# Weight sums of the 7-product blocks formed on VectorE instead of by accumulating transfers, with later transposes and another order of steps

## The chip, the cores and the metric

The kernel runs on one core of one Trainium2 chip, as one launch. The metric is the device time of that launch in microseconds (us), here the median of three runs. All data are fp32. The products use the fp32r form, in which each operand is split into a high part and the rest, so that one product of two tiles is three matmuls.

## The reference

Two transformer-like blocks run one after the other on 256 tokens of width 1024. Cut to what matters here:

```python
x = x + 0.5 * swiglu(rms_norm(x, g), w_gate, w_up, w_down)     # four of these, FF = 2816
x = x + mixer_1(x)        # sparse attention and pooling
x = x + mixer_2(x)        # spatial gating and short convolution
# order: swiglu, mixer_1, swiglu | swiglu, mixer_2, swiglu, final norm

def swiglu(x, w_gate, w_up, w_down):
    return (jax.nn.silu(x @ w_gate) * (x @ w_up)) @ w_down
```

The change touches the four swiglu stages, called FFN 1 to 4 below, and the choice of PSUM bank for transposes in the two mixers.

## The kernel before, in words

**An FFN stage** (`ffn`, L318) has three parts. The gate and up products are made for eleven groups of 256 columns, in pairs: five groups of 512 columns (numbers 0 to 4) and one of 256 (number 5). The gated result is transposed into the tile `act`, and the down product (`down`, L368) reads `act`.

**Weights come in chunks** of 128 x 2048 (1 MB). `weights` (L62) loads one through SP's queue into one of two `raw` buffers. `parts` and `split` (L70, L76) make the high part on ScalarE (ACT, `whi`, L77) and the rest on VectorE (DVE, `wlo`, L78). There are three buffers of each, so the splitting runs at most three chunks ahead of the matmuls. `mm3` (L80 to L85) then runs three matmuls per pair of tiles, on L83, L84 and L85. L84 is the first that needs `wlo`, and L85 the first that needs the low part of the activations. A plain chunk is 24 matmuls of 512 columns.

**Plain groups** (`eight`, L344) take a chunk per step. Group 5 takes two chunks and groups 2 and 4 take four. After the last one, `silu` runs on ACT (`sg`, L330) and `gated` multiplies on DVE (`pr`, L338). Then `turned` (L204) transposes `pr` on TensorE (L210) and splits the result into `act` on ACT and DVE. `turned` is put off by `later(f, n)`: each step of the order ends with `flush`, which takes 2 off n after a plain step and 1 after a block step, and runs f where nothing is left.

**Blocks of seven products** (`seven`, L358, and `quad`, L154) do groups 1 and 3. They multiply a 2 x 2 arrangement of weight chunks w11, w12, w21, w22 with seven products instead of eight. A product is 12 matmuls of 512 columns, one product per step. The activation sums are made once per FFN (`combined`, L133, which uses two of the four `block` buffers for its own data and splits into `xc`). Four weight sums are needed:

- w12 + w22 and w11 + w12: made by accumulating transfers (L175). A second DMA from HBM is added to the chunk that is in SBUF already. These and the plain loads of `block` (L151) are issued by GpSimd's (POOL's) queue.
- then + w22 and + w21 onto the latter: made on DVE (L192, L195).

`block` has four buffers, so the second block's loads wait until the first block gives buffers back, and the third and fourth load of the first block wait for `combined`.

**The order of the steps** is written out by hand in `ORDER` (L36): `e` is group 5, `a` the block of group 1, `2` and `4` the groups 2 and 4, `b` the block of group 3, `d` the down product. In what follows a1 to a7 and b1 to b7 are the steps of the blocks. The queue of each engine follows this order on the whole, but not strictly: an instruction may stand ahead of one of an earlier step.

**The end of an FFN's gate part:** the last act chunk (group 3) becomes ready last, so the first half of `down` takes its chunks in the order 0, 1, 2, 4, 5, 3 (L374). Chunk 5 is half as long.

**In the mixers** (`mixer1` L442, `mixer2` L695) `ps` (L58) goes round all eight PSUM banks, while `turned` and the transposes in `add` (`pair`, L266) take one of the three banks tagged `tmp`.

Of the kernel before, what the change touches and what calls it, by code (L numbers as in the profile page):

```python
# [13 lines left out]
ALU = mybir.AluOpType  # L14
# [3 lines left out]
P = 128  # L18
T = 256
# [13 lines left out]
MASKED = -1.0e30  # L33
WARM = 14

ORDER = "eaeaa2a2aa2a244bb4bb4bdbdbdddddddddd"  # L36


class Block:
# [14 lines left out]

    def bank(self, tag, shape=(P, 512)):
        return self.psum.tile(list(shape), F32, tag=tag, name=tag, bufs={"acc": 5, "tmp": 3}[tag])

    def ps(self, shape=(P, 512)):  # L58
        self.banks += 1
        return self.bank("acc" if self.banks % 8 < 5 else "tmp", shape)  # L60
# [93 lines left out]
    def quad(self, pool, b, x, xc):  # L154


        nc, tt = self.nc, self.nc.vector.tensor_tensor
        of_x = lambda c, t: lambda k: self.both(x[:, 4 * c + k, :, t * P : t * P + P])
        of_xc = lambda i: lambda k: self.both(xc[:, 4 * i + k, :, :])

        def product(left, w):
            ps = self.bank("tmp")
            for k in range(4):
                c = slice(k * 512, k * 512 + 512)
                self.mm3(ps, left(k), (w[0][:, c], w[1][:, c]), k == 0, k == 3)
            return ps

        p = lambda tag: pool.tile([P, 512], F32, tag=tag, name=tag)

        def copy(ps, tag):  # L170
            y = p(tag)
            nc.scalar.activation(y, ps, AF.Copy)
            return y

        more = lambda w, src: nc.gpsimd.dma_start(w, src, accum_op=ALU.add)  # L175
        (b11, b12), (b21, b22) = b
        w11, w12, w22, w21 = self.block(b11), self.block(b12), self.block(b22), self.block(b21)
        more(w12, b22)
        y11 = copy(product(of_x(0, 0), self.parts(w11)), "p1")
        more(w11, b12)  # L180
        yield
        p7 = copy(product(of_xc(2), self.parts(w12)), "p7")
        yield
        y12 = copy(product(of_xc(3), self.parts(w22)), "p3")
        yield
        y21 = p("p2")
        tt(y21, product(of_x(1, 0), self.parts(w21)), y11, op=ALU.add)
        y11, v = y21, y11
        yield
        p5 = copy(product(of_xc(0), self.parts(w11)), "p5")  # L190
        yield
        tt(w11, w11, w22, op=ALU.add)  # L192
        tt(v, product(of_xc(1), self.parts(w11)), v, op=ALU.subtract)
        yield
        tt(w11, w11, w21, op=ALU.add)  # L195
        w = self.parts(w11)
        ps = product(of_x(1, 1), w)
        tt(p7, p7, v, op=ALU.add)
        tt(v, v, p5, op=ALU.add)
        tt(p5, p7, p5, op=ALU.add)  # L200
        tt(p7, ps, p7, op=ALU.subtract)
        return y11, p7, y12, v, p5

    def turned(self, dst, x, k):  # L204

        for t in range(2):
            n = x[t].shape[1] // P
            pt = self.bank("tmp", (P, 4, P))
            for i in range(n):
                self.nc.tensor.transpose(pt[:, i, :], x[t][:, i * P : i * P + P], self.ident)  # L210
            s = slice(t * P, t * P + P)
            self.split(dst[:, k : k + n, 0, s], dst[:, k : k + n, 1, s], pt[:, :n, :])
# [37 lines left out]
    def add(self, accs, f, scale, following, tiles=(0, 1)):  # L250

        nc = self.nc
        s = slice(f * 512, f * 512 + 512)
        for t in tiles:
            x = self.X[t][:, s]
            nc.vector.scalar_tensor_tensor(x, accs[t], scale, x, op0=ALU.mult, op1=ALU.add)
        if following is None:
            return
        for t in tiles:
            self.squares(t, f)  # L260
        if following == "final_norm_2":
            return
        if f == 0:
            self.hT = self.big.tile([P, KD, 2, T], F32R, tag="hT", name="hT")

        def pair(k):  # L266
            pt = self.bank("tmp", (P, 2, T))
            for i in range(2):
                for t in range(2):
                    nc.tensor.transpose(pt[:, i, t * P : t * P + P], self.X[t][:, (k + i) * P : (k + i) * P + P], self.ident)  # L270
            for i in range(2):
                self.feed(k + i, pt[:, i, :], following)

        for k in (4 * f, 4 * f + 2):
            self.later(lambda k=k: pair(k), 3)
# [42 lines left out]
    def ffn(self, n, following, first=False):  # L318
        nc, a = self.nc, self.a
        gu, d, d_end = a[f"gu{n}"], a[f"d{n}"], a[f"de{n}"]  # L320
        with self.stage(4), self.tc.tile_pool(name="act", bufs=1) as pool:
            act = pool.tile([P, KF, 2, T], F32R, tag="act", name="act")
# [11 lines left out]
            def gated(j, sgs, us):  # L334
                prs = []
                for t in range(2):
                    pr = self.work.tile([P, 512], F32, tag="pr", name="pr", bufs=4)[:, : us[t].shape[1]]
                    nc.vector.scalar_tensor_tensor(pr, us[t], r[:, t : t + 1], sgs[t], op0=ALU.mult, op1=ALU.mult)  # L338
                    prs.append(pr)
                self.later(lambda: self.turned(act, prs, 4 * j), 2)  # L340

            two = lambda: [self.bank("acc") for _ in range(2)]

            def eight(j):  # L344
                G = two()
                self.token_major(G, gu[2 * j], 512, 0)
                yield
                self.token_major(G, gu[2 * j], 512, 1)
                sgs = silu([x[:, :T] for x in G] if j == 5 else G)
                if j < 5:  # L350
                    yield
                    U = two()
                    self.token_major(U, gu[2 * j + 1], 512, 0)
                    yield
                    self.token_major(U, gu[2 * j + 1], 512, 1)
                gated(j, sgs, [x[:, T:] for x in G] if j == 5 else U)

            def seven(j):  # L358
                y11, y21, y12, x, y22 = yield from self.quad(pool, [[gu[2 * j + i, c] for i in range(2)] for c in range(2)], self.hT, xc)

                def rest():
                    tt = nc.vector.tensor_tensor
                    tt(y12, y12, x, op=ALU.add)
                    gated(j, silu([y11, y21]), [y12, y22])

                self.later(rest, 3)

            def down():  # L368
                for f in range(2):
                    accs = two()  # L370
                    w = lambda c: self.weights(d[f, c] if c < 5 else d_end[f])
                    rows = lambda c, w, last, **k: self.rows(accs, w, act, 4 * c, 4 if c < 5 else 2, last, **k)
                    split = f == 1 and following == "final_norm_2"
                    order = (0, 1, 2, 4, 5, 3) if f == 0 else range(4 if split else 6)  # L374
                    for c in order:
                        if f or c:
                            yield
                        rows(c, w(c), 15 if f == 0 else KF - 1)
                    if split:
                        ws = [w(4), w(5)]  # L380
                        for t in range(2):
                            for c in (4, 5):
                                rows(c, ws[c - 4], KF - 1, tiles=[t])
                            self.add(accs, f, 0.5, following, [t])
                    else:
                        self.add(accs, f, 0.5, following)
# [12 lines left out]
            if not first:  # L399
                self.token_major(U, gu[1], 512, 1)  # L400
            gated(0, silu(G), U)
            combined = self.combined(xc, self.hT)
            next(combined)

            steps = {"a": seven(1), "b": seven(3), "2": eight(2), "4": eight(4), "e": eight(5), "d": down()}
            for step in ORDER:
                next(steps[step], None)
# [34 lines left out]
    def mixer1(self, following):  # L442
# [225 lines left out]
        def out(t, O):  # L668
# [4 lines left out]
            self.split(mT[0][:, :, 0, s], mT[0][:, :, 1, s], pt)  # L673

        ET = turned(0)
        pls = means()
        O = attend(0, ET)
        pooled(pls)
        ET = turned(1)
        mT[0] = self.m1.tile([P, 4, 2, T], F32R, tag="L1", name="mT")  # L680
        project(1, 0)
# [281 lines left out]
```

## Time and profile before

| what | us |
|---|---|
| median of three runs | 1137.19 (1135.1 to 1139.62) |
| profiled execution, its own time | 1135.03 |
| its span, first to last instruction | 1133.3 |
| TensorE busy with matmuls | 1081.6 |
| VectorE busy | 758.3 |
| ScalarE busy | 576.0 |

The busy time of TensorE includes overlap of one matmul with the next, so the distance between the starts of two matmuls says more than the length of one. The mean granted clock of TensorE over the span was 0.983 of full speed.

The FFNs lie at about 0 to 200, 305 to 505, 505 to 700 and 930 to 1133 us. In each, the first steps of the order begin some 25 us in.

### The profile page before, as it was taken

The page shows a single profiled execution, that of the slowest core. Times are in us where ns is not written, and L with a number is a line of the kernel's source. Part 1 is how long each engine was busy: PE and PEld are TensorE (multiplying, and loading weights), DVE is VectorE, ACT ScalarE, POOL GpSimd, SP SyncE. Part 2 cuts the span into 40 slices and gives each one's busy share as a digit, 9 for nine tenths or more (in the row PEclk, how much of TensorE's full clock was granted, in tenths as well). Part 3 has the DMA queues.
Part 4 walks back from the last instruction along what each step waited for, and adds up shares of the span by engine and source line. Part 5 has one row for each costly group of instructions (what it writes and reads, how often), then busy time and mean ns, then how long its engine had stood idle before and what let it go on. Part 6 is the DMA issues. An engine that isn't in the chain of part 4 may idle for free.

```text
span 1133.3 us, 12907 instructions
## 1 busy us (share of the span) xinstructions
PE 1081.6 (95%) x5182; PEld 900.8 (79%) x5182; DVE 758.3 (67%) x780; ACT 576.0 (51%) x657; POOL 51.2 (5%) x85
## 2 busy tenths in 40 slices
PE   9898999899998899999889999999999999889996
PEld 7677888778887688888768878999888878767885
DVE  6685875597575769646776855687545557666953
ACT  7545543577454464544646454533444445546442
POOL 1100000120010000001000000000000001000000
PEclk9999999999998999999989999999999999999999
DMA  9956365633386743659574565454545438674362
GB/s 355 284 176 226 112 231 187 251 112 113 112 290 192 259 115 132 224 188 313 179 260 112 206 229 208 175 189 174 184 176 178 169 120 281 201 253 119 130 223 74
DMA packets 34956, 218.54 MB, mean 193 GB/s; under 512 B 4609, under 2 KB 5009, under 8 KB 10321
## 3 DMA queue, kind: packets, MB, share of 16 engines
q1 hardware_dynamic: 26784, 164.20, 39.8%
q0 software_dynamic: 7680, 52.98, 16.1%
q8 instruction: 40, 0.66, 0.2%
q10 hardware_dynamic: 432, 0.55, 0.1%
q14 instruction: 20, 0.16, 0.0%
HBM read 216.66 MB, written 1.05 MB: 192 GB/s over the span
## 4 chain that ended last, share of the span: by engine, by line
PE 70%; DVE 10%; DMA 10%; issue 5%; ACT 4%; POOL 0%; SPq 0%; POOLq 0%; ACTq 0%; DVEq 0%
PE acc L85 16%; PE acc L83 16%; PE acc L84 16%; PE tmp L83 6%; PE tmp L84 6%; PE tmp L85 6%; DVE wlo L78 6%; DMA block<-in_gu 5%; DMA raw<-in_gu 4%; ACT whi L77 3%; PE tmp L210 2%; PE acc L91 1%; DMA raw<-in_d 1%; DVE xc L78 1%; DVE block L192 1%
## 5 line engine op out<-in xcount | busy, mean ns | idle before, releaser
L78 DVE TENSOR_TENSOR wlo<-raw,whi 128x2048 fp32r<-128x2048 f32 (+1 forms) x127 | 282.2, 2222 | 175.4 <-ACT whi L77 175.4
L77 ACT ACTIVATE whi<-raw 128x2048 fp32r<-128x2048 f32 (+1 forms) x127 | 236.3, 1860 | 244.3 <-PE acc L85 106.8
L78 DVE TENSOR_TENSOR wlo<-block,whi 128x2048 fp32r<-128x2048 f32 (+2 forms) x99 | 198.5, 2013 | 100.4 <-ACT whi L77 100.3
L85 PE MATMUL acc<-whi,hT 128*128 128x512 f32 (+1 forms) x608 | 238.1, 392 | 3.2 <-DVE hT L223 3.2
L83 PE MATMUL acc<-whi,hT 128*128 128x512 f32 (+1 forms) x608 | 240.0, 396 | 0.5 <-ACT whi L77 0.4
L84 PE MATMUL acc<-wlo,hT 128*128 128x512 f32 (+1 forms) x608 | 238.4, 392 | 1.3 <-DVE wlo L78 1.3
L77 ACT ACTIVATE whi<-block 128x2048 fp32r<-128x2048 f32 (+2 forms) x99 | 166.7, 1691 | 107.5 <-PE acc L85 27.3
L84 PE MATMUL acc<-wlo,act 128*128 128x512 f32 x352 | 137.1, 389 | 0.6 <-DVE wlo L78 0.6
L83 PE MATMUL acc<-whi,act 128*128 128x512 f32 x352 | 137.6, 391 | 0.0
L85 PEld LDWEIGHTS acc<-whi,hT 128*128 128x128 f32 x608 | 115.8, 190 | 27.0 <-DVE hT L223 3.6
L85 PE MATMUL acc<-whi,act 128*128 128x512 f32 x352 | 136.9, 392 | 0.1
L84 PEld LDWEIGHTS acc<-wlo,hT 128*128 128x128 f32 x608 | 116.0, 191 | 24.6 <-DVE wlo L78 2.1
L83 PEld LDWEIGHTS acc<-whi,hT 128*128 128x128 f32 x608 | 116.2, 191 | 24.3 <-ACT hT L222 0.8
L85 PEld LDWEIGHTS acc<-whi,act 128*128 128x128 f32 x352 | 66.1, 188 | 15.2 <-DVE act L78 1.6
L84 PEld LDWEIGHTS acc<-wlo,act 128*128 128x128 f32 x352 | 66.1, 188 | 14.6 <-DVE wlo L78 1.0
L83 PEld LDWEIGHTS acc<-whi,act 128*128 128x128 f32 x352 | 66.1, 188 | 13.3
L83 PE MATMUL tmp<-whi,hT 128*128 128x512 f32 x144 | 57.2, 397 | 4.3 <-ACT whi L77 4.3
L84 PE MATMUL tmp<-wlo,hT 128*128 128x512 f32 x144 | 56.2, 390 | 0.0
L85 PE MATMUL tmp<-whi,hT 128*128 128x512 f32 x144 | 56.1, 390 | 0.0
L84 PE MATMUL tmp<-wlo,xc 128*128 128x512 f32 x128 | 52.7, 412 | 1.6 <-DVE wlo L78 1.6
L83 PE MATMUL tmp<-whi,xc 128*128 128x512 f32 x128 | 53.5, 418 | 0.0
L210 PE MATMUL tmp<-ident,pr 128*128 128x128 f32 x176 | 27.9, 296 | 26.6 <-DVE pr L338 26.6
(249 smaller groups left out, 1390.6 us busy)
## 6 DMA issues: line engine op xcount, KB each, us to landing
raw<-in_gu SPq DMA_DIRECT2D x52, 1024.0 KB, 4.9
block<-in_gu POOLq DMA_DIRECT2D x48, 1024.0 KB, 8.5
raw<-in_d SPq DMA_DIRECT2D x40, 1024.0 KB, 4.8
raw<-in_de SPq DMA_DIRECT2D x8, 512.0 KB, 3.5
block<-in_w_out SPq DMA_DIRECT2D x4, 1024.0 KB, 4.9
raw<-in_w_out SPq DMA_DIRECT2D x4, 1024.0 KB, 5.1
block<-in_w_cx SPq DMA_DIRECT2D x4, 1024.0 KB, 4.9
raw<-in_w_cx SPq DMA_DIRECT2D x4, 1024.0 KB, 5.0
```

Source lines behind the costliest of these rows:

```text
L77: self.nc.scalar.activation(hi, x, AF.Copy)
L78: self.nc.vector.tensor_tensor(lo, x, hi.bitcast(F32), op=ALU.subtract)
L83: mm(ps, lhsT=a[0], rhs=b[0], start=start, stop=False)
L84: mm(ps, lhsT=a[0], rhs=b[1], start=False, stop=False)
L85: mm(ps, lhsT=a[1], rhs=b[0], start=False, stop=stop)
L91: self.nc.tensor.matmul(ps, lhsT=a, rhs=b, start=start, stop=stop)
L192: tt(w11, w11, w22, op=ALU.add)
L210: self.nc.tensor.transpose(pt[:, i, :], x[t][:, i * P : i * P + P], self.ident)
```

## The change

The two accumulating transfers of each block are gone. The sums w11 + w12 and w12 + w22 are formed by two DVE instructions directly after the first product's split, and w12 is loaded first. The transposes of a gated result are put off by 4 instead of 2. The order of the steps runs both chunks of group 5 ahead of the first block's first product and spreads the blocks' steps otherwise. In the mixers, transposes take a bank from the round of eight.

```diff
-ORDER = "eaeaa2a2aa2a244bb4bb4bdbdbdddddddddd"
+ORDER = "eeaa2a2aa2a2a44bb4b4bbdbdbdddddddddd"
...
+    def side(self, shape):
+        return self.ps(shape) if self.spare else self.bank("tmp", shape)
...
-        more = lambda w, src: nc.gpsimd.dma_start(w, src, accum_op=ALU.add)
         (b11, b12), (b21, b22) = b
-        w11, w12, w22, w21 = self.block(b11), self.block(b12), self.block(b22), self.block(b21)
-        more(w12, b22)
+        w12, w11, w22, w21 = self.block(b12), self.block(b11), self.block(b22), self.block(b21)
         y11 = copy(product(of_x(0, 0), self.parts(w11)), "p1")
-        more(w11, b12)
+        tt(w11, w11, w12, op=ALU.add)
+        tt(w12, w12, w22, op=ALU.add)
         yield
         p7 = copy(product(of_xc(2), self.parts(w12)), "p7")
...
     def turned(self, dst, x, k):
-            pt = self.bank("tmp", (P, 4, P))
+            pt = self.side((P, 4, P))
...
         def pair(k):
-            pt = self.bank("tmp", (P, 2, T))
+            pt = self.side((P, 2, T))
...
-                self.later(lambda: self.turned(act, prs, 4 * j), 2)
+                self.later(lambda: self.turned(act, prs, 4 * j), 4)
```

## Rows read from the trace of the kernel before

**Rows 1.** The page's first part: busy us of each engine, share of the span, number of instructions.

```profile
PE 1081.6 (95%) x5182; PEld 900.8 (79%) x5182; DVE 758.3 (67%) x780; ACT 576.0 (51%) x657; POOL 51.2 (5%) x85
```

**Rows 2.** The waits of TensorE's matmuls over the whole span: who waited for whom, us in total, times, longest.

```profile
PE tmp L210 <- DVE pr L338: 26.6, 10, 4.1
PE tmp L83 <- ACT whi L77: 4.3, 4, 1.1
PE acc L85 <- DVE hT L223: 3.2, 1, 3.2
...
PE tmp L84 <- DVE wlo L78: 1.6, 4, 0.4
```

**Rows 3.** Busy time by stretch: from:to, its length, busy us of each engine with the number of its instructions, granted TensorE clock (1.00 is full speed), share of the DMA engines, GB/s. The first stretch is the down product of FFN 1, the other four hold the blocks of FFN 1 to 4.

```profile
110.00:200.00 90.00, 90.00 (x410) 74.44 (x409) 59.59 (x43) 44.83 (x39) 0.00 (x0) 1.00 0.50 175
...
20.00:110.00 90.00, 79.87 (x347) 64.47 (x346) 62.77 (x53) 46.53 (x43) 8.05 (x12) 0.96 0.74 251
...
329.00:405.00 76.00, 69.16 (x297) 55.45 (x296) 52.20 (x39) 38.15 (x34) 6.23 (x9) 0.93 0.69 218
...
520.00:600.00 80.00, 72.59 (x311) 58.82 (x310) 54.68 (x40) 41.17 (x36) 6.75 (x10) 0.94 0.71 223
...
954.00:1030.00 76.00, 66.72 (x298) 53.94 (x297) 52.67 (x39) 37.98 (x35) 6.23 (x9) 0.98 0.69 216
```

**Rows 4.** Timeline of TensorE in FFN 2, at the end of group 2: start us, length, line, operation, tiles, count, and in brackets the idle time before with what ended it.

```profile
391.02 0.39 PE L84 MATMUL acc<-wlo,hT 128*128 128x512 f32 x1
391.25 0.39 PE L85 MATMUL acc<-whi,hT 128*128 128x512 f32 x1
393.77 0.66 PE L210 MATMUL tmp<-ident,pr 128*128 128x128 f32 x4 [2.13 <-DVE pr L338]
...
395.55 0.63 PE L84 MATMUL acc<-wlo,hT 128*128 128x512 f32 x1
395.98 0.63 PE L85 MATMUL acc<-whi,hT 128*128 128x512 f32 x1
```

**Rows 5.** The first of the two large waits in FFN 2: one piece of the chain that ended last (start, us, what), then lines of the timeline of ACT and TensorE.

```profile
331.37 11.80 DMA block<-in_gu
...
343.25 1.92 ACT L77 ACTIVATE whi<-block 128x2048 fp32r<-128x2048 f32 x1 [3.34 <-DMA block<-in_gu]
345.07 0.46 ACT L330 ACTIVATE sg<-acc,rstd 128x256 f32<-128x256 f32 x1
...
347.95 1.12 PE L210 MATMUL tmp<-ident,pr 128*128 128x128 f32 x4 [3.23 <-DVE pr L338]
```

**Rows 6.** Transfers, from issue to landing: the accumulating ones of L175 (least, median, longest us), and from the page the medians of the block loads (L175's included) and of the loads into `raw`.

```profile
DMA to landing us min/median/max: 7.7/10.6/17.6
...
raw<-in_gu SPq DMA_DIRECT2D x52, 1024.0 KB, 4.9
block<-in_gu POOLq DMA_DIRECT2D x48, 1024.0 KB, 8.5
```

**Rows 7.** The second large wait in FFN 2: one piece of the chain that ended last, then a line of the timeline of ACT.

```profile
378.34 9.77 DMA raw<-in_gu
...
388.21 1.92 ACT L77 ACTIVATE whi<-raw 128x2048 fp32r<-128x2048 f32 x1 [8.29 <-DMA raw<-in_gu]
```

**Rows 8.** The first of the two small waits inside the first block of FFN 2 (step a6, right behind a5): lines of the timeline of DVE, ACT and TensorE.

```profile
367.16 2.28 DVE L192 TENSOR_TENSOR block<-block 128x2048 f32<-128x2048 f32 x1
...
369.54 1.92 ACT L77 ACTIVATE whi<-block 128x2048 fp32r<-128x2048 f32 x1 [1.05 <-DVE block L192]
...
371.49 2.29 DVE L78 TENSOR_TENSOR wlo<-block,whi 128x2048 fp32r<-128x2048 f32 x1 [2.04 <-ACT whi L77]
...
373.83 0.50 PE L84 MATMUL tmp<-wlo,xc 128*128 128x512 f32 x1 [0.41 <-DVE wlo L78]
```

**Rows 9.** Groups of instructions by line and shape on DVE: count, busy us in total, mean ns of one, idle time of the engine before them.

```profile
L78 DVE TENSOR_TENSOR act<-tmp,act 128x512 fp32r<-128x512 f32 x40 | 26.0, 683 | 5.2 <-ACT act L77 5.2
...
L192 DVE TENSOR_TENSOR block<-block 128x2048 f32<-128x2048 f32 x8 | 18.3, 2282 | 0.0
...
L338 DVE SCALAR_TENSOR_TENSOR pr<-acc,rstd,sg 128x512 f32<-128x512 f32 x24 | 17.7, 745 | 4.1 <-PE acc L85 4.1
```

**Rows 10.** Where the first block begins in FFN 2: lines of the timeline of DVE (the splits of two chunks) and of TensorE (the transposes behind the first `e` chunk).

```profile
331.14 2.28 DVE L78 TENSOR_TENSOR wlo<-block,whi 128x2048 fp32r<-128x2048 f32 x1
333.34 2.28 DVE L78 TENSOR_TENSOR wlo<-raw,whi 128x2048 fp32r<-128x2048 f32 x1
...
335.51 1.03 PE L210 MATMUL tmp<-ident,pr 128*128 128x128 f32 x8
```

**Rows 11.** Busy time by stretch, columns as in rows 3: all block steps of FFN 2, and the 15 us of them in which DVE is fullest.

```profile
329.00:465.00 136.00, 129.16 (x569) 105.34 (x568) 97.91 (x70) 70.64 (x60) 6.23 (x9) 0.96 0.58 185
435.00:450.00 15.00, 15.00 (x68) 12.43 (x67) 14.80 (x11) 8.02 (x6) 0.00 (x0) 1.00 0.20 70
```

**Rows 12.** The transposes of group 3 and the chunk that needs them, in FFN 2: lines of the timeline of TensorE, ACT and DVE.

```profile
460.77 1.04 PE L210 MATMUL tmp<-ident,pr 128*128 128x128 f32 x8
...
461.56 0.48 PE L83 MATMUL acc<-whi,act 128*128 128x512 f32 x1
...
462.84 1.07 ACT L77 ACTIVATE act<-tmp 128x512 fp32r<-128x512 f32 x2
...
465.18 1.28 DVE L78 TENSOR_TENSOR act<-tmp,act 128x512 fp32r<-128x512 f32 x2
```

## The prediction

> **What bounds the kernel now.** I read the page's engine shares first. TensorE is busy for 95% of the span, VectorE (DVE) for 67%, ScalarE (ACT) for 51% [rows 1]. So TensorE sets the time, and the question is how much of its time is not work. The view of its waits answers this: 26.6 us in ten waits of its transposes of a gated result (L210) for DVE's `pr`, and 4.3 + 1.6 us in waits of block products for a split [rows 2]. All lie in the four stretches that hold the block steps; the down product beside them runs 90.00 of 90 us [rows 3].
>
> Each large wait has a second price. Ahead of one, matmuls of 512 columns start 0.23 us apart; behind it they start 0.43 us apart [rows 4], the granted clock having gone from 2.4 to 1.2 GHz after TensorE stood still. The four stretches have granted clocks of 0.96, 0.93, 0.94 and 0.98 over 90, 76, 80 and 76 us [rows 3]: 3.6 + 5.3 + 4.8 + 1.5 = 15.2 us lost. The sum on the table is 26.6 + 5.9 + 15.2 = 47.7 us.
>
> Next, why `pr` is late. In FFN 2 the first large wait follows group 5. The accumulating transfer for w12 + w22 takes 11.80 us. ACT's queue has the split of that chunk ahead of group 5's silu (`sg`), so ACT stands until 343.25 and `sg` starts at 345.07, with TensorE waiting for `pr` until 347.95 [rows 5]. These transfers take 10.6 us in the median and 17.6 at most, against 4.9 for a load into `raw` [rows 6]. The second large wait follows group 2: a `raw` load takes 9.77 us beside the next block's loads and a sum transfer, and ACT idles 8.29 us for it [rows 7]. In both, the transposes stand directly behind the last matmul of their group, so the whole chain of matmul, `sg`, `pr` is in TensorE's way. The small waits: step a6 follows a5 at once, but needs DVE's addition (367.16), ACT's split (369.54) and DVE's split (371.49) in turn [rows 8]; a7's wait is alike.
>
> **How much room is there?** Where TensorE never waits, its weight loads are busy 74.44 of 90 us, 82.7% [rows 3]; over the span they are busy 79%, 900.8 us [rows 1]. 900.8 / 0.827 = 1089 us, 44 under the span, close to the 47.7. The Trainium skill (Perfetto Trace Analysis, Identifying the Most-Contended Engine) says to judge room by the busy share of LDWEIGHTS, not by that of matmuls. Read plainly, that would be 21% of the span, 233 us. The rows differ: in this kernel 83% is already full.
>
> **The change, part by part.**
>
> *Later transposes (4 for 2).* Group 2's now come behind a7 and one plain chunk: 12 + 24 matmuls at 0.23 [rows 4] are 8 us, against waits of 4.1 us at most [rows 2]. Group 5's come behind a1 and a2, 5.5 us. So all ten waits go: -26.6, and with them the clock's -15.2. If that cover fails, a wait returns at its present price.
>
> *Order.* Behind a5, a6 and a7 there now stands a plain chunk (5.5 us) for a chain of 2.3 + 1.9 + 2.3 = 6.5 us [rows 8] that starts before the product ahead has ended. -5.9.
>
> *Accumulating transfers.* 16 MB less comes from HBM. I count no gain beyond the waits. POOL loses 16 issues and gains none; the loads in its queue wait, as now, for buffers, and w12 merely goes first.
>
> *Sums on DVE.* Per block two additions like L192's, 2.28 us long [rows 9], but 2.2 from start to start [rows 10]: 4.4 us, 35 in all. Over FFN 2's block steps DVE is busy 97.9 of 136 us [rows 11]. With 8.8 more, and the waits and slow clock out (76 - 69.2 + 5.3 = 12 [rows 3]), that is 106.7 of 124, or 86%. In its fullest 15 us DVE worked 14.80 and TensorE still never waited [rows 11]. So mostly it is cover. Two places are tight:
>
> - a2. The second `e` chunk ends 24 x 0.227 = 5.45 us after 335.51, at 341.0; eight transposes and a1 make it 344.6 [rows 10]. DVE has two chunks split by 335.6 [rows 10]; the sums take until 340.0, ACT's split 1.9, DVE's 2.3: 344.3, just in time. Then `pr` and `act` of group 5 and 0 (some 2.2 us of DVE) and the next split (2.3) end at 348.8, where TensorE wants it at 348.0: 0.8, taken as 1.0.
> - b2. From the start of a7 to b2 TensorE has 2.7 + 5.5 + 0.8 + 5.5 + 2.7 = 17.2 us. DVE's list: two `pr` pairs at 0.75, a pair of `act` at 0.68 [rows 9], five 512-wide additions at about 0.65, three splits at 2.2, the sums: 3.0 + 1.4 + 3.2 + 6.6 + 4.4 = 18.6, and ACT's 1.9 before the last split. 20.5 is 3.3 too long if nothing can go before or after, and nothing if the additions and `act` can. I take 1.5.
>
> The bounds for each place are 0 (the chunk buffers allow running ahead) and 4.4 (both sums bare).
>
> What queues behind the waiting sum: w12 + w22 makes DVE wait for w22's load, whose buffer comes from `combined`. It is due some 8.5 us [rows 6] after it is issued, and the second `e` chunk gives it 5.5 us more than now.
>
> *Group 3's transposes* move too: from before chunk 5 of the down product to directly ahead of chunk 3, which reads them. Now 12 matmuls lie between: transposes at 460.77, ACT's `act` at 462.84, DVE's until 466.46, both behind the next chunk's splits [rows 12]. If queues are free, the first half needs 0.4 + 0.6 + 0.7 = 1.7 us from 460.77, 0.9 after the transposes end. If not, up to 466.46 - 461.56 = 4.9, less the 1.8 us of eight matmuls that need no low part: 3.1. I take 0.9, since the next chunk's split can be over by then. Bounds 0.2 and 3.1.
>
> *Banks in the mixers.* No transposes there wait for a bank now; the one wait of size is 3.2 us for `hT` [rows 2]. I take 0, between -3.2 and +4 (a chain like that at either mixer's end).
>
> **Sum.** 1135.0 (this execution; span 1133.3 and 1.7 around it) - 47.7 + 4 x (1.0 + 1.5 + 0.9) = 1100.9. The median of the runs is 2.2 above this execution: 1103 us.
>
> **The rivals.**
>
> *The loads stay late.* The second block's loads still run beside `raw` loads, so the 9.8 us load was theirs and not the sum transfer's doing. Then the wait behind group 2 stays, as a wait for the next chunk's split. I take half of the 26.6 us for it, 13 (in FFN 2 it is 2.13 [rows 4] beside 3.23 [rows 5]), and half the clock's loss, 7: 1123. For it: several loads overlap there. Against it: one transfer of the rush is gone, and the second block's loads go out one by one as a2, a5, a6 and a7 give buffers back. The same size results if the queues as built keep some transposes where they are, since an instruction may stand ahead of its step [rows 5]. Chance 0.20.
>
> *DVE becomes the bound, and it is slower than before.* DVE's one queue takes the sums ahead of the split that TensorE wants next. In the first block of each FFN it also stands for w22's load as ACT does now for the sum: 4 x (3.2 wait [rows 5] + 1.7 clock + 4.4) = 37; in the second blocks 4 x (4.4 + 1.7) = 24. The 1.7 is 3.4 us at half clock, about one slow run of [rows 4]. 1135.0 - 47.7 + 61 + 4 x 0.9 + 2.2 = 1154. It decides once a block pays over 47.7 / 8 = 6.0 us with its clock loss. The Trainium skill (Perfetto Trace Analysis, Optimizing Scalar/DVE Operations) speaks for this side: it advises to move work off a full DVE, and this change does the opposite. For it: 14.80 of 15. Against it: TensorE didn't wait even then [rows 11], and w22 is there early. Chance 0.08. Halfway, a gain and a loss that cancel, about 1135: 0.06.
>
> **How the numbers follow.** Forecast, 1090 to 1112: 0.63. Late loads, 1112 to 1130: 0.20. Cancelled: 0.06. Slower: 0.08. Below 1090 (all new costs zero give 1089): 0.03. The range 1089 to 1124 takes in the forecast with its bounds (all new costs zero at the low end; one of the tight places at its upper bound in each FFN, 4 x 3.4 = 14, gives 1117) and the likelier part of the late loads. A measurement of this kernel tells about 0.5% (5.7 us) from no change. Faster by more: 0.63 + 0.20 + 0.03 and a little of the cancelled case, 0.87. Within: 0.06. Slower: 0.07.
>
> **What would show it right or wrong.** Right: no waits of L210 for `pr` above 1 us; granted clock near 1.00 in the four stretches; DVE busy 35 us more; block loads landing in 5 to 8 us; small waits for `wlo` behind a2 and b2, and for `act` ahead of chunk 3. Wrong: an idle gap of DVE ahead of the new additions that ends with a landing; waits above 2 us for `wlo`; a stretch whose clock stays at 0.93.

## The result and the profile after

The changed kernel takes 1093.68 us in the median (1091.25 to 1099.57), against 1137.11 us for the kernel before (four runs of each): a ratio of 0.9625, with a 95% interval of 0.9582 to 0.9668. That is 43.4 us less; the forecast was 1103, with a range of 1089 to 1124. The profiled execution took 1093.17 us, its span 1091.4, or 41.9 less than before.

The page's first part for the changed kernel, columns as in [rows 1]:

```profile
PE 1066.6 (98%) x5182; PEld 891.9 (82%) x5182; DVE 792.3 (73%) x796; ACT 574.9 (53%) x657; POOL 36.8 (3%) x69
```

DVE has 16 instructions and 34.0 us more, POOL 16 instructions fewer. TensorE is busy for 98% of the span. Its waits in the changed kernel, which answer to [rows 2] (lines are 2 or 3 further down in the new file, so L83 to L85 are L86 to L88, and L210 is L212):

```profile
PE acc L86 <- ACT whi L80: 9.9, 10, 1.7
PE acc L88 <- DVE hT L225: 3.3, 1, 3.3
PE acc L87 <- DVE wlo L81: 1.7, 3, 1.1
PE tmp L94 <- POOL mhalf L836: 1.0, 1, 1.0
PE tmp L94 <- ACT rel L496: 0.7, 1, 0.7
```

No wait of the transposes for `pr` is left, and none of a block product for a split. The ten waits of the first line are new but for one at the kernel's start (1.12 us, where the kernel before has one of 0.4): eight stand behind a1 and b1, one of 0.78 us in the down product of FFN 3. The stretches that hold the blocks, columns as in [rows 3]:

```profile
20.00:108.00 88.00, 84.76 (x385) 69.07 (x384) 76.18 (x59) 53.45 (x49) 4.46 (x8) 1.00 0.59 222
...
318.00:391.00 73.00, 71.71 (x327) 58.76 (x326) 63.65 (x44) 41.53 (x36) 2.65 (x5) 1.00 0.51 189
...
500.00:580.00 80.00, 77.47 (x354) 63.54 (x353) 68.48 (x48) 47.23 (x42) 3.18 (x6) 1.00 0.51 184
930.00:1003.00 73.00, 70.98 (x326) 58.16 (x325) 62.60 (x44) 44.14 (x40) 2.12 (x4) 1.00 0.44 161
```

The granted clock is 1.00 in all four. DVE now works 63.65 of 73 us there, where it worked 52.20 of 76.

Where the new waits come from, in FFN 2. Timeline of DVE and ACT (both sums, the split of w12, the next chunk's high part), then of TensorE behind a1 and behind b1:

```profile
325.99 2.29 DVE L181 TENSOR_TENSOR block<-block 128x2048 f32<-128x2048 f32 x1
328.31 2.29 DVE L182 TENSOR_TENSOR block<-block 128x2048 f32<-128x2048 f32 x1
...
330.64 1.91 ACT L80 ACTIVATE whi<-block 128x2048 fp32r<-128x2048 f32 x1 [1.10 <-DVE block L182]
...
333.77 1.92 ACT L80 ACTIVATE whi<-raw 128x2048 fp32r<-128x2048 f32 x1
...
335.74 0.73 PE L86 MATMUL acc<-whi,hT 128*128 128x512 f32 x2 [0.44 <-ACT whi L80]
336.31 0.47 PE L86 MATMUL tmp<-whi,xc 128*128 128x512 f32 x1
...
390.83 0.73 PE L86 MATMUL acc<-whi,hT 128*128 128x512 f32 x2 [0.86 <-ACT whi L80]
```

The sums run without a wait for a load. ACT must wait for the second one to split w12, and the next plain chunk's split stands behind that in ACT's queue. TensorE's queue has matmuls of that chunk (335.74) ahead of a2 (336.31), so they are what waits. Behind b1 the order in both queues is the same, but ACT does not stand idle for the sum there: a silu fills its queue until the sum is done.

### The profile page after: what moved, and what is told of

Same layout as the page of the kernel before. It is cut to its first block, busy times and chain, and to the rows that moved or that the text cites. A ratio compares the mean times of both kernels' runs of the same rounds, so it can differ in the third digit from the quotient of the medians.

```text
span 1091.4 us, 12871 instructions
## 1 busy us (share of the span) xinstructions
PE 1066.6 (98%) x5182; PEld 891.9 (82%) x5182; DVE 792.3 (73%) x796; ACT 574.9 (53%) x657; POOL 36.8 (3%) x69
## 4 chain that ended last, share of the span: by engine, by line
PE 83%; DMA 5%; DVE 4%; ACT 4%; issue 3%; SPq 0%; POOLq 0%; POOL 0%; ACTq 0%; DVEq 0%
PE acc L86 19%; PE acc L88 19%; PE acc L87 19%; PE tmp L87 7%; PE tmp L88 7%; PE tmp L86 7%; ACT whi L80 3%; DMA raw<-in_gu 2%; DVE wlo L81 2%; PE tmp L212 1%; PE acc L94 1%; DMA block<-in_gu 1%; DVE block L182 1%; DVE block L181 1%; DMA qg<-in_q_norm 1%
## 5 line engine op out<-in xcount | busy, mean ns | idle before, releaser
L86 PE MATMUL acc<-whi,hT 128*128 128x512 f32 (+1 forms) x560 | 218.9, 393 | 9.1 <-ACT whi L80 9.1
L88 PE MATMUL acc<-whi,hT 128*128 128x512 f32 (+1 forms) x560 | 218.1, 390 | 3.3 <-DVE hT L225 3.3
L87 PE MATMUL acc<-wlo,hT 128*128 128x512 f32 (+1 forms) x560 | 219.1, 391 | 1.3 <-DVE wlo L81 1.3
L86 PE MATMUL acc<-whi,act 128*128 128x512 f32 x352 | 138.3, 393 | 0.8 <-ACT whi L80 0.8
L88 PE MATMUL acc<-whi,act 128*128 128x512 f32 x352 | 135.9, 389 | 0.0
L86 PEld LDWEIGHTS acc<-whi,hT 128*128 128x128 f32 x560 | 105.5, 190 | 33.5 <-ACT whi L80 11.9
L88 PEld LDWEIGHTS acc<-whi,hT 128*128 128x128 f32 x560 | 106.2, 190 | 24.5 <-DVE hT L225 3.5
L87 PEld LDWEIGHTS acc<-wlo,hT 128*128 128x128 f32 x560 | 106.2, 190 | 23.3 <-DVE wlo L81 2.5
L86 PEld LDWEIGHTS acc<-whi,act 128*128 128x128 f32 x352 | 66.1, 188 | 15.3 <-ACT act L80 1.3
L88 PEld LDWEIGHTS acc<-whi,act 128*128 128x128 f32 x352 | 66.1, 188 | 13.9
L86 PE MATMUL tmp<-whi,hT 128*128 128x512 f32 x192 | 75.8, 395 | 0.0
L88 PE MATMUL tmp<-whi,hT 128*128 128x512 f32 x192 | 74.8, 390 | 0.0
L87 PE MATMUL tmp<-wlo,hT 128*128 128x512 f32 x192 | 74.8, 389 | 0.0
L86 PE MATMUL tmp<-whi,xc 128*128 128x512 f32 x128 | 50.4, 394 | 0.0
L87 PE MATMUL tmp<-wlo,xc 128*128 128x512 f32 x128 | 50.2, 392 | 0.0
L88 PE MATMUL tmp<-whi,xc 128*128 128x512 f32 x128 | 49.9, 390 | 0.0
```

Of the source, the lines that this page charges most:

```text
L86: mm(ps, lhsT=a[0], rhs=b[0], start=start, stop=False)
L87: mm(ps, lhsT=a[0], rhs=b[1], start=False, stop=False)
L88: mm(ps, lhsT=a[1], rhs=b[0], start=False, stop=stop)
```

## The experiments

Two theories were to be told apart. **A:** a large wait is the chain matmul, silu, gating standing directly in front of the transposes; slack in TensorE's queue cures it, whatever delays the chain. **B:** the accumulating transfers are the cause, and the transposes only show it. Each part of the change was made alone on the kernel before, and undone alone in the changed kernel. The part "sums on DVE" includes that w12 is loaded first; the two were not tried apart. All ratios are against the kernel before on the same chip.

| part | alone | ratio, interval | all but this part | ratio, interval |
|---|---|---|---|---|
| later transposes | 1126.44 us | 0.9893, 0.9852 to 0.9933 | 1119.66 us | 0.9838, 0.9799 to 0.9876 |
| sums on DVE | 1128.69 us | 0.9897, 0.9862 to 0.9932 | 1111.82 us | 0.9758, 0.9722 to 0.9794 |
| order of steps | 1138.52 us | 0.9997, 0.9981 to 1.0013 | 1127.16 us | 0.9895, 0.9853 to 0.9937 |
| banks in the mixers | 1133.25 us | 0.9945, 0.9926 to 0.9963 | 1096.34 us | 0.9625, 0.9592 to 0.9658 |

**Later transposes alone.**

```diff
-                self.later(lambda: self.turned(act, prs, 4 * j), 2)
+                self.later(lambda: self.turned(act, prs, 4 * j), 4)
```

> The kernel before with one edit: the transposes of a gated result put off by 4 instead of 2. Theory A (the wait is the chain matmul, silu, gating directly behind a group, so slack in TensorE's queue cures it whatever delays the chain): nearly all of the 26.6 us of waits of the transposes and the 15 us of clock go; what stays is a wait of a2 for the late accumulated w12 (1 to 3 us per FFN) and about 1 us for group 3's transposes: 1105 to 1115 us. Theory B (the accumulating transfers are the cause, the transposes only show it): the waits move to the block products, as waits for a split of 3 to 4 us that bring the clock down as before: 1125 to 1137 us.

1126.44 us, between the two. Its waits, as in [rows 2], show why:

```profile
PE tmp L83 <- ACT whi L77: 11.6, 10, 3.1
PE tmp L84 <- DVE wlo L78: 7.8, 7, 1.8
PE acc L84 <- DVE wlo L78: 4.4, 5, 1.6
...
PE tmp L210 <- DVE pr L338: 0.7, 1, 0.7
```

Of the transposes' 26.6 us 0.7 are left, as A has it. But the first three lines hold 23.8 us of other waits, where the kernel before has 7.8 (5.9 of them in [rows 2]): block products wait for the split of the accumulated w12, and plain chunks for a late load, as B has it. In all, TensorE's waits fell by 8 us only, from 41.8 to 33.9. The rest of the gain goes with the clock, whose mean over the span is 0.992 in this execution, against 0.983 before. In the other three runs it was 0.983 to 0.988, and they took 1125.49 to 1133.17 us.

**Sums on DVE alone.** The edit is that of `quad` in the diff above.

> The kernel before with one edit: the two sums of each block as additions on VectorE, no accumulating transfers. Theory A: the transposes still stand directly behind their group, and silu and gating take 2 to 3 us even when nothing is late: eight to ten waits stay, shorter, with their clock losses, and the sums cost a little: 1122 to 1137 us. Theory B: the large waits go with the transfers, 1100 to 1112 us.

1128.69 us, inside A's range. The transposes still wait (the line of `turned` is L209 here), ten times, for 15.9 us instead of 26.6:

```profile
PE tmp L209 <- DVE pr L337: 15.9, 10, 2.4
PE acc L83 <- ACT whi L77: 6.9, 5, 1.7
PE tmp L83 <- ACT whi L77: 4.4, 4, 1.1
```

**The order alone.** The edit is the line of `ORDER`.

> The kernel before with one edit: the new order of steps. Both theories: the small waits inside the first block go (5.9 us); the large ones stay, since transposes still follow their group at once and the accumulating transfers are there. A: 1125 to 1135 us. B: the blocks begin later, so the sum transfers have 5.5 us more time and the first large wait of each FFN goes too: 1110 to 1122 us.

1138.52 us, no difference, and worse than both theories had it. The small waits inside the first block are gone, as both had it; others stand in their place. One piece of the chain in FFN 2, then ACT and TensorE:

```profile
332.42 10.58 DMA block<-in_gu
...
343.02 1.91 ACT L77 ACTIVATE whi<-block 128x2048 fp32r<-128x2048 f32 x1 [4.08 <-DMA block<-in_gu]
...
345.46 1.91 ACT L77 ACTIVATE whi<-raw 128x2048 fp32r<-128x2048 f32 x1
...
347.42 1.22 PE L83 MATMUL acc<-whi,hT 128*128 128x512 f32 x2 [6.09 <-ACT whi L77]
```

The blocks begin later, but the sum transfer does not begin earlier: it stands in POOL's queue behind a load that waits for the same buffers, and is issued at 332.42 where it was at 331.37 [rows 5]. It lands at 343.0. ACT's queue has the split of that chunk ahead of a plain one, so a plain chunk waits 6.09 us in the transposes' place.

**Banks in the mixers alone.** `turned` and `pair` use `side`, as in the diff above.

> The kernel before with one edit: in the mixers, transposes take a bank from the round of eight. The prediction counted 0 for it, between -3.2 and +4. If the waits of 1.6 and 1.2 us in front of the second mixer's output product, which are absent from the trace of the changed kernel, went by this edit: 1132 to 1135 us. If they went by a shift in time: 1136 to 1138 us.

1133.25 us, so this part does act. Between 890 and 940 us this kernel's TensorE has no wait for an engine; in the one with all parts but this the waits of 1.6 and 1.2 us are there:

```profile
PE acc L86 <- ACT mT L80: 1.6, 1, 1.6
PE acc L88 <- DVE mT L81: 1.2, 1, 1.2
```

So it is in every trace: the kernels without this part have both waits (before, the other three parts alone, all but this part), and those with it have neither. The time fell by 5.4 us (4 to 8 by the interval), more than these 2.8; what the rest is stays open.

**All parts but the later transposes.**

> The changed kernel with one part undone: transposes put off by 2 again. Theory A (slack in TensorE's queue is what cures the waits): about ten waits of 2 to 3 us come back with most of the clock loss: 1115 to 1130 us. Theory B (the accumulating transfers were the cause): at most 8 us over the changed kernel, 1094 to 1102 us.

1119.66 us, inside A's range, but not by A's way: the transposes wait 2.8 us in all, and plain chunks 20.9 us for ACT:

```profile
PE acc L86 <- ACT whi L80: 20.9, 12, 3.5
PE tmp L212 <- DVE pr L340: 2.8, 7, 1.7
```

In FFN 2 ACT's queue then has the split of w12 waiting for the second sum, a silu and an `act` behind it, and the next plain chunk's split last, so TensorE does not get its weights:

```profile
337.90 1.91 ACT L80 ACTIVATE whi<-block 128x2048 fp32r<-128x2048 f32 x1 [1.28 <-DVE block L182]
339.72 0.46 ACT L332 ACTIVATE sg<-acc,rstd 128x256 f32<-128x256 f32 x1
340.07 0.37 ACT L80 ACTIVATE act<-tmp 128x256 fp32r<-128x256 f32 x1
340.34 1.91 ACT L80 ACTIVATE whi<-raw 128x2048 fp32r<-128x2048 f32 x1
```

**All parts but the sums.**

> The changed kernel with one part undone: the accumulating transfers are back, VectorE has 35 us less. Theory A: with the later order the transfers have time to land, so the cost is small and the waits of a2 and b2 for VectorE (some 9 us in all) go: 1085 to 1100 us. Theory B: the transfers land late again and the block products wait for them: 1105 to 1125 us.

1111.82 us, inside B's range. It is mostly plain chunks that wait (10.9 us for ACT, in four waits), and block products less (4.8). One piece of the chain, then ACT and TensorE in FFN 2:

```profile
326.73 10.66 DMA block<-in_gu
...
337.41 1.91 ACT L80 ACTIVATE whi<-block 128x2048 fp32r<-128x2048 f32 x1 [2.88 <-DMA block<-in_gu]
...
340.18 1.91 ACT L80 ACTIVATE whi<-raw 128x2048 fp32r<-128x2048 f32 x1
...
342.14 0.49 PE L86 MATMUL acc<-whi,hT 128*128 128x512 f32 x1 [4.57 <-ACT whi L80]
```

Even with the later order and the later transposes the accumulated chunk is late, and the plain chunk behind it in ACT's queue pays.

**All parts but the order.**

> The changed kernel with one part undone: the old order of steps. Both theories: the small waits of a6 and a7 return (6 us), and the first block begins a chunk earlier, so a2 waits for the sums and for w22's load by 2 to 5 us in each FFN: 1105 to 1120 us. If the order matters for the small waits alone: 1099 to 1102 us.

1127.16 us, more than either reading. The small waits are back (0.64 and 1.1 us in each FFN). In FFN 2 to 4, a2 waits 0.86 to 1.20 us for DVE's split, not the 2 to 5 expected. In FFN 1 a1 waits 5.10 us for a block load that landed 8.09 us after its issue, the second of the block, which is w11 since w12 goes first. And there is a wait that was on no list, once in each FFN: a product of the second block waits for the split of `act`. The first line is of its waits, the others of the timeline of DVE and TensorE in FFN 2:

```profile
PE tmp L86 <- DVE act L81: 14.5, 4, 4.0
...
407.23 1.28 DVE L81 TENSOR_TENSOR act<-tmp,act 128x512 fp32r<-128x512 f32 x2
...
407.97 0.79 PE L86 MATMUL tmp<-whi,xc 128*128 128x512 f32 x1 [3.76 <-DVE act L81]
408.56 0.63 PE L87 MATMUL tmp<-wlo,xc 128*128 128x512 f32 x1
408.98 0.63 PE L88 MATMUL tmp<-whi,xc 128*128 128x512 f32 x1
```

No data lead from `act` to that product. What they share is the three `tmp` banks of PSUM: the transposes took two, b1 the third, and b2 needs the first again, which is held until DVE has read it. The product starts when the first of DVE's two `act` instructions (0.68 us each [rows 9]) is over, which fits; that this is the link is argued from the tiles and the time, not tried. Behind the wait matmuls start 0.42 us apart, at half clock.

**All parts but the banks.**

> The changed kernel with one part undone: transposes in the mixers take a tmp bank again. If the 3 us of waits ahead of the second mixer's output product went by this part: 1096 to 1098 us; if not, 1093 to 1095 us.

1096.34 us against 1093.68, with the same ratio of 0.9625 to the kernel before. The waits came back as shown above, 2.8 us in one trace; the time does not tell it apart.

**The price of the additions.** The changed kernel with two lines taken out.

```diff
-        tt(w11, w11, w12, op=ALU.add)
-        tt(w12, w12, w22, op=ALU.add)
```

> The changed kernel without the two additions of each block on VectorE (the sums w11 + w12 and w12 + w22 are left out, the loads stay): 35 us less work on VectorE. It prices the added work where it stands now. If the waits behind a1 (0.4 to 1.7 us) and behind b1 (0.9 us) in each FFN are the sums' doing: they go, and nothing else moves: 1084 to 1089 us. If they come from ACT's or VectorE's queue whatever is in it, or if the added work costs time elsewhere that shows as no wait: 1091 to 1095 us for the first, below 1083 us for the second.

1083.46 us, ratio 0.9516 (0.9489 to 0.9543). The ten waits for `whi` are two, 1.8 us:

```profile
PE acc L87 <- DVE wlo L81: 2.5, 3, 1.8
PE acc L86 <- ACT whi L80: 1.8, 2, 1.2
```

Neither of the two stands behind a1 or b1, so those waits are the additions' doing. The time lies just under the range for that. The changed kernel has a second reading of 1094.39 us, on this run's chip (**Tables later**, below), and beside it the 35 us of additions cost 10.9 us. Some 8 of these show as waits for `whi` (9.9 us against 1.8); the rest shows as no wait.

**A chunk between a1 and a2.**

```diff
-ORDER = "eeaa2a2aa2a2a44bb4b4bbdbdbdddddddddd"
+ORDER = "eea2aa2aa2a2a44b4bb4bbdbdbdddddddddd"
```

> The changed kernel with the order of steps edited once more: a plain chunk now stands between a1 and a2 and between b1 and b2, and the pairs a2 a3, a4 a5, b2 b3, b4 b5 follow each other. If the waits behind a1 and b1 are the chain sum, sum, split before a2 and b2: they go, 1085 to 1090 us. If a later pair then waits in their place: 1091 to 1098 us.

1087.07 us, ratio 0.9549 (0.9522 to 0.9576), better than both kernels. The waits behind a1 and b1 are gone, and in their place a pair waits no longer than 0.24 us in each FFN; one in FFN 1 for the first `e` chunk has grown from 1.1 to 2.1 us:

```profile
PE acc L87 <- DVE wlo L81: 4.2, 7, 2.1
PE acc L88 <- DVE hT L225: 2.2, 1, 2.2
PE acc L86 <- ACT whi L80: 1.0, 1, 1.0
```

**Tables later.** Outside the change: the longest wait left, 3.3 us, is in the first mixer, where DVE stands for the load of a small table. Cut from the edit below: `mixer1_tables` issues its loads up to the first `next`, and its six products at the second.

```diff
-        self.mixer1_tables()
+        tables = self.mixer1_tables()
+        next(tables)
...
         products("q", 1)
-
+        next(tables, None)
```

> The changed kernel with one edit outside the change: in the first mixer, VectorE's six small products for the tables stand behind the second chunk of q instead of ahead of it (the loads stay where they are). VectorE stood 4.62 us for the load of one of them, and TensorE 3.28 us behind it with 6.8 us of half clock after. If the table load is the cause: 3.3 + 3.4 = 6.7 us less, 1086 to 1089 us. If VectorE then waits elsewhere: 1091 to 1095 us.

1094.39 us, ratio 0.9613 (0.9585 to 0.9641): no difference. DVE's timeline shows that the edit did not act. The products stand in DVE's queue where they stood, behind the same load:

```profile
201.55 0.29 DVE L441 TENSOR_TENSOR qC<-cosq,qg 128x128 f32<-128x128 f32 x1 [4.12 <-DMA qg<-in_q_norm]
```

So whether that load is the cause stays open. The run serves as a second reading of the changed kernel.

**Both.**

> Both edits, of the order and of the tables, on the changed kernel. If they act on different waits, as the trace has it: the sum of the two gains, 12 to 15 us, 1079 to 1083 us. The bound from the matmuls' starts is near 1075 us.

1087.84 us, ratio 0.9557 (0.9531 to 0.9584): the order's gain alone. The sum of two gains did not come, as the tables' edit brought none.

## Why the prediction was right

**The reading of the bound held.** TensorE's time was waits and slow clock in four stretches, and the change took just these: the transposes' 26.6 us, the small waits' 5.9 and the clock's 15.2 are all gone. The floor of 1089 us from the weight loads was near but not hard: with a chunk between a1 and a2 the span is 1084.9 us.

**The new costs were 9 us, not 13.6, and of another kind.** By the waits, behind a1: 1.28, 0.44, 1.67 and 1.15 us in FFN 1 to 4, mean 1.1 where 1.0 was taken. Behind b1: 0.86 in each, where 1.5 was taken. Group 3's transposes: a wait above 0.1 us in FFN 3 only, 0.78 + 0.40, where 0.9 was taken in each. The first two were sized near the mark, but by a wrong step. The prediction summed up DVE's work and had a2, b2 or the chunk behind wait for their own `wlo`, and named such waits as a sign of being right. None came: all eight are waits for ACT's `whi`, of a plain chunk whose split stands behind that of w12. That the size came out near is luck.

**The banks were not 0, but their size is not settled.** The prediction looked for transposes waiting for a bank and found none. What the edit took away are two waits of other work, 2.8 us. With it, TensorE runs matmuls behind the transposes (lines of TensorE and ACT, changed kernel):

```profile
882.13 0.47 PE L86 MATMUL acc<-whi,mT 128*128 128x512 f32 x1
...
883.36 0.58 ACT L80 ACTIVATE mT<-acc 128x512 fp32r<-128x512 f32 x1
```

They start before ACT has split the new `mT`, so they must be of the other, older `mT`. By the times the part is worth 5.4 us alone and nothing that can be told when undone. The bounds of -3.2 and +4 hold for the waits; the 5.4 lies outside.

Together, by the waits: -47.7 + 9.2 - 2.8 = -41.3, against -41.9 by the spans. Forecast was -34.1. The difference is in these two terms.

**What the prediction had wrong is who does it.** It gave the whole 41.8 us of transposes and clock to the later transposes, 5.9 to the order, and to the missing transfers no gain beyond. Alone, the later transposes gain 12 us and the order nothing; with all else in place, undoing the order costs 31 to 33 us, and bringing the transfers back 15 to 18 (first by the ratios, then by the medians). Its total came out because all four parts were made at once; its terms by part do not match what the parts do alone. Neither A nor B holds alone: the chain to `pr`, the late sum and the adjacent steps delay the same queue, ACT's, or in the run without the order, by what the tiles suggest, the `tmp` banks. Take away one, and the next plain chunk or product waits for the other. The gains of the four parts alone sum to 1.07 + 1.03 + 0.03 + 0.55 = 2.7% of the time; together they are worth 3.75%.

**The rivals.** Late loads did not occur, and the reason given for them was wrong: it held that the 9.8 us load [rows 7] came from `raw` and `block` loads side by side and not from the sum transfer. From issue to landing the longest `raw` load beside FFN 2's blocks takes 11.7 us in the kernel before, 7.2 with the sums on DVE alone, 7.1 in the changed kernel, and 8.8 when the transfers come back. A DVE bound did not either, though DVE is the nearest thing to one: over FFN 2's block steps it is busy for 111.61 of 133 us, 84%, where 86% was worked out, and its additions cost 10.9 us of 35. They are not free, but not by a full DVE.

## What to carry to other kernels

Where several late inputs feed one engine's queue, the wait is charged to one of them, and curing that one shows the next: price such edits together, and test them by undoing one at a time too, since alone they may show nothing (the order: 0.03% alone, 2.7% in company). When a dependent pair of additions and a split stand between two adjacent steps of the busiest engine, put independent work between the steps before counting the additions; here that was worth 7 us for a change of one string. A source line moved later need not move in an engine's queue: look at the queue first.

## What the runs showed of the hardware

**Waits and the clock.** The eight waits of 0.44 to 1.67 us in the four stretches of the changed kernel leave their granted clock at 1.00; the wait of 3.76 us above was followed by starts 0.42 us apart, which is half clock. The length of a wait alone does not tell: in the kernel before, one of 3.23 us (the transposes at 1017.63) was followed by starts 0.23 us apart, at full clock, and in the kernel without the additions one of 1.82 us (at 31.70) by starts 0.43 us apart. So not every large wait had the second price that the prediction gave it.

**Accumulating transfers.** One of 1 MB took 10.6 us from issue to landing in the median of the 16 in the kernel before (7.7 to 17.6), 9.4 with the order alone (7.8 to 13.8) and 9.6 with all parts but the sums (7.8 to 14.5). The 32 plain loads of the same queue take 5.4 us in the median in the changed kernel (4.9 to 11.2). How much of the difference is the accumulating and how much the traffic beside it, no run here shows.
